# Loading the down-projection weights for their sums behind each pair's own weight loads, in a two-layer encoder step

## The chip, the cores and the metric

The kernel runs on one core of one Trainium2 chip. The metric is the device time of one launch in microseconds. The core has five engines with an instruction queue each: PE (TensorE, matmuls), DVE (VectorE), ACT (ScalarE), POOL (GpSimd) and SP (SyncE), which here issues all the transfers. Each engine works through its own list in the listed order and waits on semaphores for the others. A scheduler lays out these lists when the kernel is built: it follows the program's order and data dependencies, and an instruction may be moved ahead of others where the scheduler expects its inputs early.

## The reference, cut to what matters

Two layers, each an attention mixer followed by a channel mixer, for 1024 prompt positions and 8 x 16 sample positions (1152 rows of 1024 values). The change touches the channel mixer:

```python
def conv_ffn(h, prev, w_up, conv_w, conv_b, w_down):
    u = h @ w_up
    ...
    y = conv_b
    for tap in range(CONV_W):
        y = y + conv_w[tap] * ue[:, tap:tap + T]
    a, g = jnp.split(y, 2, axis=-1)
    out = (jax.nn.gelu(g) * a) @ w_down
    return out, ue[:, T:]
...
    f, conv_rows = conv_ffn(h, None if prompt else state_conv[l], w_up[l], conv_w[l], conv_b[l], w_down[l])
    x = layer_norm(DEEPNORM_ALPHA * x + (1 + g_f) * f, ln_g[l, 1], ln_b[l, 1])
```

`w_up` has 2 x 2816 columns, that is 22 blocks of 128 for `a` and 22 for `g`; `w_down` has 22 blocks of 128 rows. All data are float32; each operand is split into a rounded part and a remainder, so every product costs three matmuls.

## The kernel before, in words

`ffn(l, ...)` is the channel mixer of layer `l` and has two stages. The **up-projection** runs over 22 pairs `j` (block `j` of `a` with block `j` of `g`). The first two (`plain`) are ordinary products. The other twenty (`spair(j)`, j = 2 to 21) use a seven-product scheme over 2 x 2 quarters (`products`): POOL forms sums of weight quarters (lines 1177 to 1180), ACT and DVE split each of seven weight operands (lines 177 and 188), PE multiplies (line 1229, 24 matmuls for each product, 168 for a pair), and DVE adds the products up out of PSUM (line 1190), ACT for two of the seven (lines 1188 and 1197). The products of a pair share three groups of PSUM banks, and products 2, 3 and 4 share one: the matmuls of the second may start only when DVE has read the first. Then the convolution follows, `conv_row`, once for `g` and once for `a`: one ACT pass (line 1316), then two long and two short DVE operations, called taps here (line 1277), and a POOL addition (line 1286). `gated` applies GELU (line 1323, ACT), multiplies (line 1324, POOL) and stores the activations (lines 1326 and 1330). After every second pair `act_sums` forms four sums of stored activations on POOL (lines 1336 to 1339, called in the pair that follows) and stores both results (line 1341); the gate row that it stores is then overwritten by the next `conv_row`, which so waits for this store.

The **down-projection** (`down`, PE line 1466) is a seven-product scheme too, and needs sums of `w_down` quarters. `weight_sums(m)`, m = 0 to 10, makes them during the up-projection: two loads of 512 KB into the pair of tiles `w0f` (line 1347), four POOL operations on 128 x 512 (lines 1348 to 1351), and two stores to DRAM (line 1353). It is called in eleven of the twenty pairs: j = 2, 3 and every even j from 4 to 20. Nothing in the code ties a sum's loads to its pair: the tile `w0f` is free as soon as the last sum is stored, so the scheduler may pull the loads, and with them the sums, as far ahead as the tile allows.

In layer 0 the up-projection also carries 64 background steps (`ada`, four matmuls of 32 x 256 at line 234 each, with a 512 KB load at line 226), and at its start a small table (`tables_b`, load at line 1650, DVE lines 1651 and 1652) and sixteen transfers that spread it in DRAM (line 1657).

`down` ends with the last layer norm, tile of 128 rows by tile. The residual rows of a tile are loaded (`rows`, line 1081) into a buffer named in `homes`; in the table of before, tiles 2, 3, 6 and 7 use again the buffers `fa` and `fb` of earlier tiles, and a load waits until the earlier tile's output is stored (line 1019).

Names in the profile: `ws` and `F` hold weights as loaded (`F` is one large scratch tile with many uses), `wh` and `wl` the split weights, `H`, `xa` and `x2r` the split activations, `w0f` the pair of tiles for the down weights, `wT` and `actS` the stored sums, `actD` the stored activations, `PS` the PSUM banks.

Of the kernel before, what the change touches and what calls it, by code (L numbers as in the profile page):

```python
# [102 lines left out]
class Trunk:  # L103
# [1140 lines left out]
    def ffn(self, l, xsrc, xdst, affs):  # L1244
        nc, I, O, H, F = self.nc, self.I, self.O, self.H, self.F
# [67 lines left out]
        def conv_row(u, j, gg, y):  # L1313
            cc = j + 22 * gg
            tap = tapper(cc)
            nc.scalar.activation(y, u[:, 2:1154], AF.Identity, bias=cw[:, cc, 3:4], scale=cw[:, cc, 2:3])  # L1316
            tap(y[:, 0:1024], u[:, 1:1025], 1)
            tap(y[:, 0:1024], u[:, 0:1024], 0)
            samples(y[:, 1024:1152], u[:, 1026:1154], cc, tap)
            rows(j, gg, u[:, 1024:1168])  # L1320

        def gated(j, ya, yg):
            nc.scalar.activation(yg, yg, AF.Gelu_apprx_tanh)
            nc.gpsimd.tensor_mul(yg, yg, ya)  # L1324
            if j % 2:
                nc.sync.dma_start(self.actD[j], yg)
                self.pend.append(j // 2)
            else:
                for r in (slice(0, 512), slice(1024, 1152)):
                    nc.sync.dma_start(self.actD[j][:, r], yg[:, r])  # L1330

        def act_sums():
            for m in self.pend:
                a11, a21 = ygate[0][:, 0:512], ygate[0][:, 512:1024]
                a12, a22 = ygate[1][:, 0:512], ygate[1][:, 512:1024]
                nc.gpsimd.tensor_add(a22, a21, a22)
                nc.gpsimd.tensor_sub(a21, a11, a21)
                nc.gpsimd.tensor_sub(a11, a22, a11)
                nc.gpsimd.tensor_sub(a12, a12, a11)
                for i in range(2):  # L1340
                    nc.sync.dma_start(self.actS[m, i], ygate[i][:, 0:1024])
            self.pend = []

        def weight_sums(m):
            b11, b12, b21, b22 = (t[:, o : o + 512] for t in self.w0 for o in (0, 512))
            for i in range(2):
                nc.sync.dma_start(self.w0[i], I["wdn"][l, 2 * m + i])
            nc.gpsimd.tensor_sub(b11, b12, b11)
            nc.gpsimd.tensor_sub(b12, b22, b12)
            nc.gpsimd.tensor_sub(b22, b22, b11)  # L1350
            nc.gpsimd.tensor_sub(b21, b22, b21)
            for i in range(2):
                nc.sync.dma_start(self.wT[l][m, i], self.w0[i])
# [13 lines left out]
        def spair(j):  # L1367
            sa, sg = self.ws.next(), self.ws.next()
            nc.sync.dma_start(sa, I["wup"][l, j])
            nc.sync.dma_start(sg, I["wup"][l, j + 22])  # L1370
            ua, ug = us.next(), us.next()
            y = []

            def after(i, q):
                if i % 2 == 0:
                    self.step(1)
                if i == 1:
                    act_sums()
                if i == 2 and j in wsum:
                    weight_sums(wsum.index(j))  # L1380
                if q == 4:
                    y.append(ygate[j % 2])
                    conv_row(ug, j, 1, y[0])

            self.products(sa, sg, ua, ug, (S1, S2, S3), p1s, sub, TT, after, "first" if j == NPL else None)
            ya = yact
            conv_row(ua, j, 0, ya)
            gated(j, ya, y[0])

        self.pend = []  # L1390
        wsum = [2, 3] + list(range(4, NFF - 1, 2))
# [9 lines left out]
        for j in range(NPL, NFF):  # L1401
            spair(j)
            if l == 0 and j == 2:
                self.tables_b(self.ws.next())
            if l == 0 and 3 <= j < 19:
                with self.tc.issue_after(self.pairmm):
                    self.skew_b(j - 3)
# [4 lines left out]
    def down(self, l, xsrc, xdst, affs, act_sums):  # L1412
        nc, I, F, H = self.nc, self.I, self.F, self.H
# [13 lines left out]
        narrow = self.ws  # L1427
        fa, fb = F[:, 4096:5120], F[:, 8320:9344]
        homes = {8: fa, 0: fb, 1: self.w0[1], 2: fa, 3: fb, 4: X2[:, 0:1024], 5: X2[:, 2048:3072], 6: fa, 7: fb}
        xs = {}  # L1430

        def rows(*ts):
# [487 lines left out]
```

## Time and profile before

| what | us |
|---|---|
| median of three runs | 2839.86 |
| lowest and highest run | 2837.35 and 2843.75 |
| the profiled execution, own time | 2844.65 |
| the profiled execution, span from first to last instruction | 2842.6 |
| first and last load for a weight sum in the trace (line 1347, layers 0 and 1) | 515.8 and 2232.6 |
| first down-projection weight cast from `w0f` (line 177) | 1064.0 |
| first and last matmul of the twenty pairs of layer 1, about | 2075 and 2565 |

The mean granted TensorE clock of the profiled execution is 0.975 of full speed. Times inside the trace count from the start of the span; 2.05 us of the execution lie outside it. The table of windows in the prediction gives, for a stretch of time, each engine's busy time and in brackets its number of instructions, then the granted clock, the DMA share and the rate. A row of the timeline gives start, duration, engine, line, operation, operands and count, and in square brackets how long the engine had been idle before it and what ended that.

### The profile page before, as it was taken

What the parts mean: (1) busy time and instruction counts of PE and PEld (TensorE: products, weight loads), DVE (VectorE), ACT (ScalarE), POOL (GpSimd) and SP (SyncE); (2) the same over time, 40 slices, a digit from 0 to 9 for tenths busy, and PEclk for the clock granted to TensorE, in tenths of its full rate; (3) what the DMA queues carried; (4) which work ended last, traced back from release to release, by engine and by line L of the source; (5) the groups of instructions that cost most, each with busy time, mean ns of one, the idle gap of its engine ahead of it and who ended that gap; (6) DMA issues with size and microseconds to landing.
All of it is one profiled execution on the core that took longest, in us unless ns stands there. A gap on an engine that the chain in (4) does not pass through costs nothing. (4 is left out here: it accounts for less than half of the span.)

```text
span 2842.6 us, 47206 instructions
## 1 busy us (share of the span) xinstructions
PE 2676.1 (94%) x17134; PEld 2356.5 (83%) x17134; DVE 2027.0 (71%) x3850; ACT 1348.0 (47%) x2752; POOL 1106.9 (39%) x808
## 2 busy tenths in 40 slices
PE   7999889889999999999899999999988999999997
PEld 5897768878999997777798888767988999997775
DVE  4376767777776684588663677668888888885578
ACT  3475724433333344455636666652443344444454
POOL 2132523678554641013421111232489855551001
PEclk9999999999999999999999999999999999999998
DMA  8656434698554447675767457854565422237664
GB/s 291 213 159 197 141 129 156 209 329 283 183 175 156 163 133 236 225 248 196 267 201 257 122 156 198 225 162 146 178 206 196 177 81 96 85 116 239 216 218 156
DMA packets 252714, 534.35 MB, mean 188 GB/s; under 512 B 40032, under 2 KB 100400, under 8 KB 252480
## 3 DMA queue, kind: packets, MB, share of 16 engines
q1 hardware_dynamic: 252480, 531.32, 56.8%
q8 instruction: 135, 2.21, 0.3%
q14 instruction: 99, 0.81, 0.1%
HBM read 391.12 MB, written 149.54 MB: 190 GB/s over the span
## 5 line engine op out<-in xcount | busy, mean ns | idle before, releaser
L1229 PE MATMUL PS<-H,wh 128*128 128x256 f32 (+1 forms) x2624 | 409.7, 299 | 0.0
L1466 PE MATMUL PS<-wh,xa 128*128 128x512 f32 x1144 | 366.9, 399 | 11.9 <-DVE F L1584 5.3
L1229 PEld LDWEIGHTS PS<-H,wh 128*128 128x128 f32 x2624 | 374.4, 193 | 0.0
L1277 DVE SCALAR_TENSOR_TENSOR F<-F 128x1024 f32<-128x1024 f32 x320 | 312.9, 1025 | 28.1 <-ACT F L1316 27.8
L177 ACT CAST wh<-F 128x512 fp32r<-128x512 f32 (+2 forms) x234 | 137.1, 594 | 316.5 <-PE PS L1229 203.7
L1190 DVE TENSOR_TENSOR F<-PS,F 128x320 f32<-128x320 f32 (+1 forms) x446 | 196.6, 451 | 123.5 <-PE PS L1229 121.6
L188 DVE TENSOR_TENSOR wl<-F,wh 128x512 fp32r<-128x512 f32 (+2 forms) x234 | 238.6, 1029 | 56.0 <-ACT wh L177 54.3
L1466 PEld LDWEIGHTS PS<-wh,xa 128*128 128x128 f32 x1144 | 215.4, 189 | 69.5 <-ACT H L177 6.1
L1229 PE MATMUL PS<-H,wl 128*128 128x256 f32 (+1 forms) x1312 | 235.4, 301 | 24.4 <-ACT F L1197 15.3
L1466 PE MATMUL PS<-wl,xa 128*128 128x512 f32 x572 | 227.0, 397 | 0.2
L1229 PEld LDWEIGHTS PS<-H,wl 128*128 128x128 f32 x1312 | 196.6, 193 | 34.3 <-ACT F L1197 16.3
L1229 PE MATMUL PS<-xa,wh 128*128 128x320 f32 (+1 forms) x1328 | 207.5, 299 | 0.0
L188 DVE TENSOR_TENSOR xa<-xa 128x640 fp32r<-128x640 f32 (+1 forms) x154 | 122.5, 801 | 112.8 <-ACT xa L177 112.3
L1229 PEld LDWEIGHTS PS<-xa,wh 128*128 128x128 f32 x1328 | 189.8, 192 | 0.0
L1065 POOL TENSOR_TENSOR F<-F 128x1024 f32<-128x1024 f32 x24 | 62.7, 2611 | 308.2 <-ACT xa L177 148.9
L177 ACT CAST xa<-xa 128x640 fp32r<-128x640 f32 (+1 forms) x154 | 104.0, 682 | 162.8 <-DMA xa<-actD 110.8
L188 DVE TENSOR_TENSOR wl<-ws,wh 128x512 fp32r<-128x512 f32 (+1 forms) x149 | 166.2, 1120 | 10.3 <-ACT wh L177 10.2
L1316 ACT ACTIVATE F<-F 128x1152 f32<-128x1152 f32 x80 | 108.0, 1351 | 114.7 <-DVE F L1190 65.7
L177 ACT CAST wh<-ws 128x512 fp32r<-128x512 f32 (+1 forms) x167 | 113.1, 685 | 102.9 <-PE PS L1229 47.1
L640 POOL TENSOR_TENSOR F<-F,x2r 64x512 f32<-64x512 f32 x62 | 79.4, 1280 | 167.9 <-DVE F L616 145.6
L1324 POOL TENSOR_TENSOR F<-F 128x1152 f32<-128x1152 f32 x44 | 123.7, 2810 | 52.1 <-DVE F L1277 40.8
L1229 PE MATMUL PS<-xa,wl 128*128 128x320 f32 (+1 forms) x664 | 122.9, 307 | 21.2 <-DVE F L1190 20.7
(346 smaller groups left out, 6287.3 us busy)
## 6 DMA issues: line engine op xcount, KB each, us to landing
ws<-in_adaw_dram SPq DMA_DIRECT2D x64, 512.0 KB
ws<-in_wup_dram SPq DMA_DIRECT2D x49, 512.0 KB
F<-in_adaw_dram SPq DMA_DIRECT2D x48, 512.0 KB
w0f<-in_wdn_dram SPq DMA_DIRECT2D x44, 512.0 KB
wT<-w0f SPq DMA_DIRECT2D x44, 512.0 KB
actS<-F SPq DMA_DIRECT2D x44, 512.0 KB
xa<-actS SPq DMA_DIRECT2D x88, 256.0 KB
F<-in_wup_dram SPq DMA_DIRECT2D x39, 512.0 KB
```

Of the source, the lines that this page charges most:

```text
L177: nc.scalar.copy(out, in_)
L188: self.eng(el).tensor_sub(lo, src, hi.bitcast(F32))
L640: self.eng("v" if last else "p").tensor_mul(on[r, q], on[r, q], rb[r, :])
L1065: self.eng(er[0]).tensor_mul(xr, x, self.lng)
L1190: nc.vector.tensor_add(d, v(ps), a if len(a.shape) == 3 else v(a))
L1229: self.pairmm = nc.tensor.matmul(ps[:, 0:m], w[a][:, k * 128 : k * 128 + 128], x(p, k, n), start=start and c == 0, stop=c == 11, skip_grou ...
L1277: nc.vector.scalar_tensor_tensor(o, u, cw[:, cc, i : i + 1], o, op0=ALU.mult, op1=ALU.add)
L1316: nc.scalar.activation(y, u[:, 2:1154], AF.Identity, bias=cw[:, cc, 3:4], scale=cw[:, cc, 2:3])
L1324: nc.gpsimd.tensor_mul(yg, yg, ya)
L1466: self.downmm = nc.tensor.matmul(ps, a[p][:, i * 128 : i * 128 + 128], w[q], start=first and c == 0, stop=last and c == 2, skip_group_chec ...
```

## The change

Three edits. In `spair`, the second weight load of the pair is kept by name, and `weight_sums` is traced inside a block that places every instruction of SP traced there behind that load in SP's queue. The block adds no semaphore and touches no other engine; POOL's sums follow only because they need the loaded data. In `down`, for layer 1 alone, the residual rows of tiles 6 and 7 get buffers of their own, `self.hf` and `self.gateS`, in place of `fa` and `fb`.

```diff
@@ def spair(j)
             nc.sync.dma_start(sa, I["wup"][l, j])
-            nc.sync.dma_start(sg, I["wup"][l, j + 22])
+            pairdma = nc.sync.dma_start(sg, I["wup"][l, j + 22]).ins
...
                 if i == 2 and j in wsum:
-                    weight_sums(wsum.index(j))
+                    with self.tc.issue_after(pairdma):
+                        weight_sums(wsum.index(j))
@@ def down
         homes = {8: fa, 0: fb, 1: self.w0[1], 2: fa, 3: fb, 4: X2[:, 0:1024], 5: X2[:, 2048:3072], 6: fa, 7: fb}
+        if l:
+            homes[6], homes[7] = self.hf, self.gateS
```

The lists change almost only inside the two up-projections and at the end of layer 1. Lines up to 1369 keep their numbers; later lines move by one to three.

POOL in the second layer, in the middle of the up-projection, around the sums of stored activations. 1179, 1177, 1178 and 1180 are the next pair's weight sums. Before:

```order
L1286 TENSOR_TENSOR F<-F 128x8x2
L1324 TENSOR_TENSOR F<-F 128x1152
L1336 TENSOR_TENSOR F<-F 128x512
L1337 TENSOR_TENSOR F<-F 128x512
L1338 TENSOR_TENSOR F<-F 128x512
L1339 TENSOR_TENSOR F<-F 128x512
L1179 TENSOR_TENSOR F<-ws 128x512
L1177 TENSOR_TENSOR F<-ws 128x512
L1178 TENSOR_TENSOR F<-F,ws 128x512
```

The same place now:

```order
L1324 TENSOR_TENSOR F<-F 128x1152
L1348 TENSOR_TENSOR w0f<-w0f 128x512
L1349 TENSOR_TENSOR w0f<-w0f 128x512
L1350 TENSOR_TENSOR w0f<-w0f 128x512
L1336 TENSOR_TENSOR F<-F 128x512
L1351 TENSOR_TENSOR w0f<-w0f 128x512
L1337 TENSOR_TENSOR F<-F 128x512
L1179 TENSOR_TENSOR F<-ws 128x512
L1338 TENSOR_TENSOR F<-F 128x512
L1177 TENSOR_TENSOR F<-ws 128x512
L1339 TENSOR_TENSOR F<-F 128x512
L1178 TENSOR_TENSOR F<-F,ws 128x512
```

Between the gate product (1324) and the second half of the activation sums (1338) stood two operations, and now stand seven. This is repeated in every second pair; before, all eleven sums stood in the first pairs.

DVE in the same pair: the last read of the pair's products from PSUM (1190, 128x5x64 and 128x4x64 are the two halves of a product), the taps of both convolutions (1277), and the first read for the next pair. Before:

```order
L1190 TENSOR_TENSOR F<-PS,F 128x5x64
L1277 SCALAR_TENSOR_TENSOR F<-F 128x1024
L1277 SCALAR_TENSOR_TENSOR F<-F 128x8x15
L1190 TENSOR_TENSOR F<-PS,F 128x4x64
L188 TENSOR_TENSOR wl<-F,wh 128x512
L1277 SCALAR_TENSOR_TENSOR F<-F 128x1024
L1277 SCALAR_TENSOR_TENSOR F<-F 128x8x14
L1277 SCALAR_TENSOR_TENSOR F<-F 128x1024
L1277 SCALAR_TENSOR_TENSOR F<-F 128x8x15
L188 TENSOR_TENSOR wl<-F,wh 128x512
L1190 TENSOR_TENSOR F<-PS,F 128x5x64
```

The same place now:

```order
L1190 TENSOR_TENSOR F<-PS,F 128x4x64
L188 TENSOR_TENSOR wl<-F,wh 128x512
L1277 SCALAR_TENSOR_TENSOR F<-F 128x1024
L1277 SCALAR_TENSOR_TENSOR F<-F 128x8x15
L1277 SCALAR_TENSOR_TENSOR F<-F 128x1024
L1277 SCALAR_TENSOR_TENSOR F<-F 128x8x15
L1277 SCALAR_TENSOR_TENSOR F<-F 128x1024
L1277 SCALAR_TENSOR_TENSOR F<-F 128x8x14
L188 TENSOR_TENSOR wl<-F,wh 128x512
L1190 TENSOR_TENSOR F<-PS,F 128x5x64
```

Both reads of the pair's last product now stand ahead of all taps, and six taps in one block stand ahead of the next pair's first read.

SP in the second layer, the same pair. 1369 and 1370 are a pair's two weight loads. Before:

```order
L1370 DMA ws<-in_wup_dram 128x1024
L1326 DMA actD<-F 128x1152
L1369 DMA F<-in_wup_dram 128x1024
L1341 DMA actS<-F 128x1024 x2
L1370 DMA F<-in_wup_dram 128x1024
```

The same place now:

```order
L1370 DMA ws<-in_wup_dram 128x1024
L1347 DMA w0f<-in_wdn_dram 128x1024 x2
L1326 DMA actD<-F 128x1152
L1353 DMA wT_105<-w0f 128x1024
L1369 DMA F<-in_wup_dram 128x1024
L1353 DMA wT_105<-w0f 128x1024
L1341 DMA actS<-F 128x1024 x2
L1370 DMA F<-in_wup_dram 128x1024
```

The two loads follow the pair's own load, and the two stores of the sum now stand ahead of the next pair's first load and ahead of the activation sums' stores.

## The prediction, made before the changed kernel ran

> **What bounds the kernel now.** I read the page first, then the table of windows over both up-projections, then PE's waits in the bad windows, then single pairs in the timeline.
>
> ```profile
> span 2842.6 us, 47206 instructions
> ...
> PE 2676.1 (94%) x17134; PEld 2356.5 (83%) x17134; DVE 2027.0 (71%) x3850; ACT 1348.0 (47%) x2752; POOL 1106.9 (39%) x808
> ```
>
> PE is the bound: it is idle for 6% of the span. The question is how much of that idle time belongs to the sums of the down weights.
>
> ```profile
> core 0: us, PE busy (x) PEld busy (x) DVE busy (x) ACT busy (x) POOL busy (x), PEclk, DMA share, GB/s
> 560.00:620.00 60.00, 48.67 (x365) 44.13 (x364) 43.17 (x52) 19.09 (x32) 42.48 (x29) 0.91 0.90 326
> 620.00:760.00 140.00, 136.25 (x1062) 124.72 (x1062) 105.27 (x135) 48.54 (x83) 111.14 (x77) 1.00 0.75 256
> 760.00:1000.00 240.00, 240.00 (x1889) 220.93 (x1889) 169.45 (x247) 91.90 (x153) 128.89 (x94) 1.00 0.49 163
> 2100.00:2260.00 160.00, 140.10 (x971) 137.80 (x972) 144.24 (x151) 54.85 (x94) 141.84 (x90) 0.94 0.53 190
> 2260.00:2540.00 280.00, 280.00 (x2101) 279.88 (x2101) 239.28 (x312) 114.93 (x198) 165.12 (x113) 1.00 0.26 93
> ```
>
> The third and fifth rows are the quiet parts: PE never idles and the clock is 1.00. They give its pace, 1889/240 = 7.87 matmuls a us in layer 0 and 2101/280 = 7.50 in layer 1, so a pair of 168 matmuls takes 22.4 us there. At these paces the other rows should have taken 365/7.87 = 46.4, 1062/7.87 = 134.9 and 971/7.50 = 129.4 us. They lost 13.6, 5.1 and 30.6 us, 49.3 us together. POOL shows the difference: 142 of 160 us busy in the bad window of layer 1, 165 of 280 in the quiet one.
>
> ```profile
> L1348 POOL TENSOR_TENSOR w0f<-w0f 128x512 f32<-128x512 f32 x8 | 14.3, 1794 | 3.4 <-DMA w0f<-in_wdn_dram 3.4
> L1349 POOL TENSOR_TENSOR w0f<-w0f 128x512 f32<-128x512 f32 x9 | 16.6, 1850 | 1.0 <-DMA w0f<-in_wdn_dram 0.9
> PE PS L1229 <- DVE F L1190: 20.1, 10, 5.6
> L1277 DVE SCALAR_TENSOR_TENSOR F<-F 128x1024 f32<-128x1024 f32 x24 | 42.2, 1760 | 0.9 <-ACT F L1316 0.8
> L1277 DVE SCALAR_TENSOR_TENSOR F<-F 128x1024 f32<-128x1024 f32 x48 | 69.9, 1457 | 10.7 <-ACT F L1316 10.7
> ```
>
> The first four rows are of 2100 to 2260, the last of 2260 to 2540. Eight of layer 1's eleven sums run in these 160 us, some seven pairs. The only releaser of PE there is DVE reading PSUM (L1190), late ten times. DVE is late because its long taps (L1277) take 1.76 us there against 1.46 later, while POOL is full.
>
> ```profile
> 2153.00 1.43 PE L1229 MATMUL PS<-xa,wl 128*128 128x320 f32 x4 [5.58 <-DVE F L1190]
> 2179.80 0.85 PE L1229 MATMUL PS<-xa,wl 128*128 128x320 f32 x4 [1.43 <-DVE F L1190]
> ```
>
> A gap also costs afterwards: behind 5.58 us idle four matmuls take 1.43 us, behind 1.43 us idle 0.85. That is why 30.6 us are lost to 20.1 us of idle time, a factor of 1.52. The Trainium skill says the same under "TensorE: Matmul & The Clock Gate", What's actually happening: the clock drops to half after an idle window of about 3.4 us. By it, eight stalls of 2 us would carry no surcharge and cost 16 us; the two rows above agree.
>
> **The change part by part.** Removed: nothing. The 44 loads, 88 POOL sums and 44 stores stay, and so do all matmuls. What moves is when they run.
>
> *Layer 1.* The first three sums stand about where they stood, and I count nothing for them. The eight others, which cost 30.6/8 = 3.8 us of PE each, move to one in every second pair. Their new price must come from a pair of the quiet part:
>
> ```profile
> 2439.05 2.68 POOL L1324 TENSOR_TENSOR F<-F 128x1152 f32<-128x1152 f32 x1 [1.53 <-DVE F L1277]
> 2444.66 1.29 POOL L1336 TENSOR_TENSOR F<-F 128x512 f32<-128x512 f32 x1 [2.93 <-DMA actD<-F]
> 2447.39 1.62 POOL L1338 TENSOR_TENSOR F<-F 128x512 f32<-128x512 f32 x1
> 2449.04 1.70 SPq L1341 DMA_DIRECT2D actS<-F  x2
> 2451.77 1.35 ACT L1316 ACTIVATE F<-F 128x1152 f32<-128x1152 f32 x1 [1.86 <-DMA actS<-F]
> 2453.15 2.58 DVE L1277 SCALAR_TENSOR_TENSOR F<-F 128x1024 f32<-128x1024 f32 x2 [1.77 <-ACT F L1316]
> 2461.12 0.48 DVE L1190 TENSOR_TENSOR F<-PS,F 128x320 f32<-128x320 f32 x1
> 2461.72 0.50 PE L1229 MATMUL PS<-xa,wl 128*128 128x320 f32 x2
> ```
>
> This is a chain with almost no slack at its end: POOL's L1338, the store of the activation sums, ACT's convolution pass, DVE's taps, DVE's read of PSUM at 2461.12 to 2461.60, and PE, which wants that bank at 2461.72. The sum is put into its head. L1324 ends at 2441.75. Now eight operations run from there to the end of L1338 (1348, 1349, 1350, 1336, 1351, 1337, 1179, 1338). At 1.5 us each, between the 1.29 and 1.62 of these rows, L1338 ends at 2453.75 in place of 2449.0: a slip of 4.7 us, of which POOL's old idle time of 2.9 has already been used up. The first tap then starts at 2457.9. In the new order six taps, a split and the read follow: three long taps of 1.457 and three short ones between 0.3 and 0.85,
>
> ```profile
> L1277 DVE SCALAR_TENSOR_TENSOR F<-F 128x120 f32<-128x120 f32 x24 | 20.4, 852 | 0.0
> L1277 DVE SCALAR_TENSOR_TENSOR F<-F 128x112 f32<-128x112 f32 x24 | 7.8, 324 | 0.0
> ```
>
> that is 4.4 + 2.0 = 6.4, with about 0.7 for the split and 0.48 for the read 7.6 us: the read ends near 2465.5. PE's new order puts seven matmuls of another product (0.9 us) ahead of the blocked ones, so PE wants the bank at 2462.65. The stall is 2.9 us; with POOL at 1.29 for each of the eight the slip is 3.1 and the stall 1.3. Bounds: nothing, if the taps are quicker too, and the old 3.8; a loss beyond that is a rival below. I take 2.0 us, the middle of the chain's two ends, and no surcharge, since the row behind 1.43 us of idle time shows next to none. Eight of them cost 16, so layer 1 gains 30.6 - 16 = 14.6 us.
>
> What waits behind the new waits: on SP the first store of a sum stands ahead of the next pair's first load and waits for L1349, done about 2444.8; the second waits for L1351 and stands ahead of the activation sums' stores, which wait longer anyway. What covers a late load is the six slots of split weights: they let the splits run up to five products of 22.4/7 = 3.2 us ahead of PE, 16 us. The first weights of the down-projection go into `w0f` too and wait for the last sum's store, but that sum belongs to pair 20, more than a pair (22.4 us) ahead; if that lead were gone, PE would wait there for one load and one split, some 4 us in each layer (the load at 561.42 below lands in 2.5).
>
> *Layer 0.* A pair has the background steps too, and here the sum falls behind the third weight sum (L1178) of every second pair:
>
> ```profile
> 863.65 1.62 POOL L1180 TENSOR_TENSOR F<-ws,F 128x512 f32<-128x512 f32 x1
> 870.39 0.22 POOL L1286 TENSOR_TENSOR F<-F 128x16 f32<-128x16 f32 x1 [5.13 <-DVE F L1277]
> 876.22 0.49 DVE L1190 TENSOR_TENSOR F<-PS,F 128x320 f32<-128x320 f32 x1
> 881.30 0.85 PE L1229 MATMUL PS<-xa,wl 128*128 128x320 f32 x4
> ```
>
> POOL sits idle for 5.13 us just there, so four operations of 1.6 us are late by little more than 1 us, and DVE's read ends 4.6 us before PE wants the bank. The cover is enough: I price these sums at nothing, and if it were gone the price would be that of layer 1, 2.0 each. So the 5.1 us of 620 to 760 come back. Of the 13.6 us of 560 to 620 the sums are one cause of several:
>
> ```profile
> 560.99 0.33 SPq L1353 DMA_DIRECT2D wT<-w0f  x1
> 561.42 0.36 SPq L1650 DMA_DIRECT2D F<-in_relf_dram  x1
> 563.91 1.04 DVE L1651 TENSOR_SCALAR F<-F 16x257 f32<-16x257 f32 x1 [6.23 <-DMA F<-in_relf_dram]
> 609.82 1.44 PE L1229 MATMUL PS<-H,wl 128*128 128x320 f32 x4 [5.66 <-DVE wl L188]
> ```
>
> The table's load stood in SP's queue behind stores of sums and DVE waited 6.23 us for it; these stores now come later. The sixteen table transfers, with a DMA share of 0.90, stay. Bounds 0 and 13.6, I take half, 7. Layer 0 gains 12.
>
> *The end.* Tiles 6 and 7 no longer wait for an older tile's store.
>
> ```profile
> 2813.78 0.32 SPq L1081 DMA_DIRECT2D F<-xd  x1
> 2817.32 1.06 ACT L1530 ACTIVATE F<-F 128x1024 f32<-128x1024 f32 x1 [11.47 <-DMA F<-xd]
> 2818.91 3.66 PE L1466 MATMUL PS<-H,xa 128*128 128x512 f32 x15
> 2823.45 0.68 DVE L1618 TENSOR_TENSOR F<-F,PS 128x512 f32<-128x512 f32 x1
> 2825.64 5.41 POOL L1017 TENSOR_TENSOR x2f<-x2f,F 128x1024 f32<-128x1024 f32 x2 [38.73 <-ACT x2f L1016]
> 2826.02 2.83 DVE L1534 CUSTOM_DVE_ANT_0 F<-F 128x512 f32<-128x512 f32 x1
> ```
>
> ACT's scaling of tile 7 held up the statistics of tiles 4 and 5 by about 2 us. But PE works until 2822.57, and DVE's last subtraction at 2823.45 cannot start earlier: 0.9 us. POOL's multiplications, beside which L1534 takes 2.83 us, may fall a little earlier too. I take 1.5, bounds 0 and 4.
>
> Sum: 14.6 + 12 + 1.5 = 28 us. The profiled execution took 2844.65, 4.8 above the median, so it would take 2816.6, and the median goes from 2839.86 to about **2812**.
>
> **The rivals.** (1) *A sum costs the same wherever it stands.* For it: each POOL operation slows some DVE operation, early or late. Against it: the same density of sums lost 30.6 us in layer 1 and only 5.1 in layer 0's second window, so slack decides. Layer 1 would gain nothing, layer 0 only 7: with the end 8.5, so 2831. The Trainium skill would have it so: "SBUF — State Buffer", SBUF: two separate sides, calls the port pair of VectorE and GpSimd an exclusive lock, held for the whole instruction, so that lost time is not shared but conserved. The taps agree in part: slowed, but not by a whole POOL operation each.
>
> (2) *The gains come back in full.* All 49.3 and 2 at the end: 2789. For it: the quiet part has DVE idle for 41 of 280 us; against it the chain above, with 0.1 us of slack.
>
> (3) *Slower: the activation sums become the bound.* The place is the chain of layer 1. With POOL at the 1.85 us that L1349 takes when crowded, and some 2, L1338 ends near 2457, a slip of 8, and PE stalls by some 6 us in each of eight pairs; with the surcharge of 1.52 that is 73 us against 30.6, so 73 - 30.6 - 13.5 = 29 lost: 2869. It decides from 3.8 + 13.5/8 = 5.5 us lost for each sum, a slip of 5.4 with the surcharge and 7.3 without (the stall is the slip less 1.8).
>
> (4) *The sums don't spread, or it doesn't matter:* the background steps could keep layer 0 late, and the early sums were not what PE waited for; 2838. Against it speaks the one releaser in layer 1.
>
> **How the numbers follow.** The forecast, 2797 to 2829, has 0.53; (1) 0.15; (2) 0.14; (3) 0.13; (4) 0.05. What a measurement here can tell is about 0.2%, 5.7 us. Rival (1) at 8.5 us is just beyond it: 0.12 faster, 0.03 same. So faster 0.79, same 0.08, slower 0.13. The range leaves out (3) and half of (2), 0.20 in all, and reaches (4): 2793 to 2838.
>
> **What would show it.** Right: in the second layer no stretch of 160 us that lost 20 us; PE's waits on L1190 once in every second pair, 1 to 3 us each, at the matmuls behind the first product of a pair; ACT's L1316 waiting for actS by some 4 us more; in layer 0 no waits after 640, and L1651 waiting less; the last load of line 1081 long before 2800. Wrong: waits on L1190 of over 4 us in every second pair (rival 3) or none (rival 2); waits on the split weights (L188) or on DMA in the middle of either up-projection, which would mean that the stores in SP's queue hold up the pairs' loads.

## The result, and the profile after

| kernel | median us | runs | ratio to before, 95% interval |
|---|---|---|---|
| before | 2841.18 | 20 | |
| the change | 2836.03 | 20 | 0.9984 (0.9973 to 0.9995) |

The change gives some 5 us, under 0.2%. The forecast was 28. The profiled execution of the change took 2832.66 us with a span of 2830.8, 11.8 less than before's span; 5.7 of that had passed ahead of the first of the twenty pairs, in code that the change leaves alone, so spans of single executions are not compared here. What is compared is the time from the first to the last pair of a layer, taken at the first L1188 of each pair (nineteen intervals).

The first and last of these rows in layer 1, before:

```profile
2090.14 0.43 ACT L1188 COPY F<-PS 128x320 f32<-128x320 f32 x1 [2.77 <-PE PS L1229]
...
2550.06 0.43 ACT L1188 COPY F<-PS 128x320 f32<-128x320 f32 x1 [0.25 <-PE PS L1229]
```

And after:

```profile
2081.03 0.43 ACT L1188 COPY F<-PS 128x320 f32<-128x320 f32 x1 [2.87 <-PE PS L1229]
...
2541.05 0.43 ACT L1188 COPY F<-PS 128x320 f32<-128x320 f32 x1 [0.23 <-PE PS L1229]
```

That is 459.9 and 460.0 us: layer 1 gained nothing, where 14.6 were forecast. In layer 0 the same count gives 499.2 and 495.2. From the last pair to the end it is 292.5 and 289.8.

The table of windows of the change, with the same columns and stretches as in the prediction:

```profile
560.00:620.00 60.00, 51.43 (x399) 47.36 (x397) 40.66 (x52) 19.06 (x33) 45.12 (x31) 0.97 0.85 310
620.00:760.00 140.00, 140.00 (x1106) 128.27 (x1099) 104.17 (x141) 52.99 (x89) 93.16 (x64) 1.00 0.58 200
760.00:1000.00 240.00, 238.95 (x1870) 220.99 (x1869) 177.59 (x248) 89.65 (x153) 159.52 (x111) 1.00 0.60 202
2100.00:2260.00 160.00, 149.08 (x1090) 146.60 (x1089) 130.17 (x165) 60.97 (x106) 113.27 (x76) 0.99 0.37 131
2260.00:2540.00 280.00, 267.93 (x1990) 264.96 (x1990) 227.16 (x296) 111.62 (x190) 188.45 (x123) 1.00 0.36 129
```

At the paces of the prediction, the fourth row loses 160 - 1090/7.504 = 14.7 us (before 30.6) and the fifth 280 - 1990/7.504 = 14.8 (before nothing). The bad stretch is gone and its loss is spread, 29.5 for 30.6. Every two steady pairs took 44.8 us before:

```profile
2416.02 0.42 ACT L1188 COPY F<-PS 128x320 f32<-128x320 f32 x1
...
2460.81 0.42 ACT L1188 COPY F<-PS 128x320 f32<-128x320 f32 x1
```

After, they take 48.0, 3.2 us more for the one sum in them:

```profile
2424.18 0.43 ACT L1188 COPY F<-PS 128x320 f32<-128x320 f32 x1 [1.00 <-PE PS L1229]
...
2472.16 0.43 ACT L1188 COPY F<-PS 128x320 f32<-128x320 f32 x1 [1.01 <-PE PS L1229]
```

The waits in layer 1 after the change (engine, line, releaser: us in total, times, longest), from 2040 to 2600:

```profile
ACT F L1316 <- POOL F L1339: 34.5, 8, 5.2
...
PE PS L1229 <- ACT F L1197: 20.4, 8, 7.7
...
PE PS L1229 <- DVE F L1190: 10.8, 18, 1.7
```

Besides the releaser that the prediction named, L1190, there is another: ACT's read of product 11 out of PSUM, L1197. One pair of the timeline shows how it becomes late:

```profile
2438.97 1.35 ACT L1316 ACTIVATE F<-F 128x1152 f32<-128x1152 f32 x1
...
2439.16 1.79 POOL L1338 TENSOR_TENSOR F<-F 128x512 f32<-128x512 f32 x1
...
2440.35 2.97 DVE L1277 SCALAR_TENSOR_TENSOR F<-F 128x1024 f32<-128x1024 f32 x2 [0.56 <-ACT F L1316]
...
2440.92 2.27 POOL L1177 TENSOR_TENSOR F<-ws 128x512 f32<-128x512 f32 x1
...
2443.14 1.33 POOL L1339 TENSOR_TENSOR F<-F 128x512 f32<-128x512 f32 x1
...
2444.50 1.35 ACT L1316 ACTIVATE F<-F 128x1152 f32<-128x1152 f32 x1 [4.09 <-POOL F L1339]
...
2445.76 0.68 ACT L1197 COPY F<-PS 128x320 f32<-128x320 f32 x2
...
2445.88 3.95 DVE L1277 SCALAR_TENSOR_TENSOR F<-F 128x1024 f32<-128x1024 f32 x4 [2.56 <-ACT F L1316]
...
2446.21 0.85 PE L1229 MATMUL PS<-H,wl 128*128 128x320 f32 x4 [1.45 <-ACT F L1197]
...
2450.36 0.48 DVE L1190 TENSOR_TENSOR F<-PS,F 128x320 f32<-128x320 f32 x1
...
2457.30 0.86 PE L1229 MATMUL PS<-x2r,wl 128*128 128x320 f32 x4 [0.82 <-DVE F L1190]
```

The wide convolution pass of the gate (the second L1316) overwrites a gate row that the last activation sum, L1339, still reads. L1339 ends 20.3 us behind the pair's first L1188 (before: 12.3). ACT has waited 4.09 us for it, and behind that pass in ACT's queue stands L1197, which frees the banks for product 21. PE waits 1.45 us, and 0.82 further on for DVE's read.

ACT's two passes of the pair have also changed places, which the lists of POOL, DVE and SP did not show. Before, the gate's pass stood first (2451.77, waiting for the store of its row) and the other second:

```profile
2456.16 1.35 ACT L1316 ACTIVATE F<-F 128x1152 f32<-128x1152 f32 x1 [2.53 <-DVE F L1190]
```

Now the other stands first (2438.97) and the late one of the gate second (2444.50).

### The profile page after: what moved, and what is told of

It reads as the page before. It is cut to its first block, busy times and chain, and to the rows that moved or that the text cites. A ratio compares the mean times of both kernels' runs of the same rounds, so it can differ in the third digit from the quotient of the medians.

```text
span 2830.8 us, 47176 instructions
## 1 busy us (share of the span) xinstructions
PE 2662.1 (94%) x17134; PEld 2341.0 (83%) x17134; DVE 2000.5 (71%) x3850; ACT 1346.4 (48%) x2752; POOL 1116.0 (39%) x808
## 5 line engine op out<-in xcount | busy, mean ns | idle before, releaser
L1469 PE MATMUL PS<-wh,xa 128*128 128x512 f32 x1144 | 367.2, 399 | 12.7 <-ACT wh L177 3.7
L1277 DVE SCALAR_TENSOR_TENSOR F<-F 128x1024 f32<-128x1024 f32 (+1 forms) x320 | 304.8, 998 | 38.2 <-ACT F L1316 37.7
L188 DVE TENSOR_TENSOR wl<-F,wh 128x512 fp32r<-128x512 f32 (+2 forms) x234 | 244.6, 1053 | 84.7 <-ACT wh L177 76.6
L1190 DVE TENSOR_TENSOR F<-PS,F 128x320 f32<-128x320 f32 (+1 forms) x446 | 194.6, 449 | 109.5 <-PE PS L1229 107.8
L188 DVE TENSOR_TENSOR xa<-xa 128x640 fp32r<-128x640 f32 (+1 forms) x154 | 120.0, 784 | 111.2 <-ACT xa L177 110.4
L1316 ACT ACTIVATE F<-F 128x1152 f32<-128x1152 f32 x80 | 108.1, 1351 | 118.8 <-DVE F L1190 46.3
L1324 POOL TENSOR_TENSOR F<-F 128x1152 f32<-128x1152 f32 x44 | 125.0, 2841 | 77.9 <-DVE F L1277 30.2
L188 DVE TENSOR_TENSOR wl<-ws,wh 128x512 fp32r<-128x512 f32 (+1 forms) x149 | 146.6, 989 | 7.9 <-ACT wh L177 7.8
L306 PE MATMUL PS<-H,w0r 128*128 128x384 f32 (+1 forms) x720 | 138.2, 342 | 0.0
```

Source lines behind the costliest of these rows:

```text
L188: self.eng(el).tensor_sub(lo, src, hi.bitcast(F32))
L306: mm = self.nc.tensor.matmul(out[:, 0:n], w[a][:, k * 128 : k * 128 + 128], H[:, p, k, s0 : s0 + n], start=i == 0, stop=i == 23)
L1190: nc.vector.tensor_add(d, v(ps), a if len(a.shape) == 3 else v(a))
L1277: nc.vector.scalar_tensor_tensor(o, u, cw[:, cc, i : i + 1], o, op0=ALU.mult, op1=ALU.add)
L1469: self.downmm = nc.tensor.matmul(ps, a[p][:, i * 128 : i * 128 + 128], w[q], start=first and c == 0, stop=last and c == 2, skip_group_chec ...
```

## Experiments

Two theories. **A, the chain:** the sum stands ahead of the activation sums on POOL, the convolution pass waits for these, and PE waits for what stands behind that pass. **B, the conserved price:** a sum costs PE about the same wherever it stands, because POOL's work slows DVE's. The diffs are against the changed kernel. "Stretch" is the time from the first to the last pair of a layer; "price" is what two steady pairs of layer 1 take above 44.8 us.

**The parts alone.** Homes only; the placing in layer 0 only; the placing in layer 1 only:

```diff
-                    with self.tc.issue_after(pairdma):
-                        weight_sums(wsum.index(j))
+                    weight_sums(wsum.index(j))
```

> Only the buffers of tiles 6 and 7 at the end of layer 1 are changed; the sums run as before. In the two traces the stretch from the last pair of layer 1 to the end is 2.7 us shorter after the change (292.5 against 289.8). If that is the homes, this kernel is 1 to 3 us (0.05 to 0.1%) faster than before, and the up-projections take what they took before (499 us from the first to the last pair in layer 0, 460 in layer 1).

```diff
+                    if l == 0:
+                        with self.tc.issue_after(pairdma):
+                            weight_sums(wsum.index(j))
+                    else:
+                        weight_sums(wsum.index(j))
...
-        if l:
-            homes[6], homes[7] = self.hf, self.gateS
```

> Only layer 0 issues the loads behind each pair's own; layer 1 and the homes are as before. Both theories: layer 0 gives 4 to 6 us (499.2 to 495.2 from the first to the last pair in the traces), so 0.9980 to 0.9986 of before. Were it nothing, the gain of layer 0 in the traces would be chance between executions.

The third has `if l == 1` in the place of `if l == 0`.

> Only layer 1 issues the loads behind each pair's own; layer 0 and the homes are as before. Both theories: no change within 2 us, 0.9993 to 1.0007, since from the first to the last pair layer 1 took 459.9 us before and 460.0 after. My forecast had 14.6 us here, 0.995.

Measured: 0.9990 (0.9975 to 1.0005), 0.9986 (0.9972 to 1.0000) and 1.0008 (0.9992 to 1.0024), that is -2.8, -4.0 and +2.3 us, none beyond doubt by itself. They add up to -4.5, the change's own 0.9984. Stretches of layer 1: 457.4 and 457.4 with the old placing, 458.2 with the new. Layer 1 is worth nothing, as its trace had said.

**The sums in the other pairs.**

```diff
-        wsum = [2, 3] + list(range(4, NFF - 1, 2))
+        wsum = [2, 3] + list(range(4, NFF - 1, 2)) if l == 0 else [2] + list(range(3, NFF, 2))
```

> As the change, but in layer 1 the sums are called in pairs 2, 3, 5, 7 ... 21 in place of 2, 3, 4, 6 ... 20, so that from pair 5 on they fall into the pairs without sums of activations. Theory A (the chain: the sum stands ahead of the activation sums on POOL, the convolution pass on ACT waits for these, and ACT's read of PSUM stands behind that pass): the waits of PE on L1197 (20.4 us in 8) and on L1190 (10.8) all but go, the pairs of the steady part take 22.4 to 22.8 us in place of 24.0, layer 1 gains 20 to 27 us, ratio to before 0.989 to 0.992. Theory B (a sum costs PE its 3.2 us wherever it stands, since POOL's work slows DVE's): layer 1 stays at 460 us from the first to the last pair, ratio 0.998 as the change.

Measured: 0.9947 (0.9928 to 0.9965), 2826.01 us, and a stretch of 446.9. Waits of PE in layer 1:

```profile
PE PS L1229 <- DVE F L1190: 9.2, 25, 1.4
PE PS L1229 <- ACT F L1197: 9.1, 3, 7.7
```

One wait of 6 to 9 us at the start of the layer is there in every kernel; of the others on L1197, 9.1 - 7.7 = 1.4 us are left of 20.4 - 7.7 = 12.7. But the ratio lies between the two expectations. The price is 1.5: out of the chain, a sum costs 1.7 us less than 3.2, and the rest has another cause.

**The sums at the same place without POOL's work.**

```diff
-            nc.gpsimd.tensor_sub(b11, b12, b11)
-            nc.gpsimd.tensor_sub(b12, b22, b12)
-            nc.gpsimd.tensor_sub(b22, b22, b11)
-            nc.gpsimd.tensor_sub(b21, b22, b21)
```

> As the change, but POOL's four operations of each weight sum are left out in both layers; the loads and stores stay, so the stored tiles hold the loaded weights and the output is not the reference's. This prices all the sums at once. If POOL's work is what the sums cost, layer 1 falls from 460 us (first to last pair) to 426 to 432, near 19 pairs of 22.4, and layer 0 from 495 by 3 to 20; ratio to before 0.980 to 0.989. If the cost is in the loads and stores in SP's queue or in the DMA share, layer 1 stays above 445 and the ratio above 0.993.

Measured: 0.9903 (0.9880 to 0.9927); stretches 490.1 and 445.5. Layer 0 came out as expected. In layer 1 the stretch fits the second expectation (above 445) and the ratio neither: the price is 1.7 with no sum computed at all. The timeline shows why:

```profile
2408.93 0.33 SPq L1349 DMA_DIRECT2D wT<-w0f  x1
...
2409.35 0.38 SPq L1326 DMA_DIRECT2D actD<-F  x1
...
2413.38 1.76 POOL L1336 TENSOR_TENSOR F<-F 128x512 f32<-128x512 f32 x1 [5.00 <-DMA actD<-F]
...
2421.33 7.60 DVE L1277 SCALAR_TENSOR_TENSOR F<-F 128x1024 f32<-128x1024 f32 x6
...
2429.99 0.86 PE L1229 MATMUL PS<-xa,wl 128*128 128x320 f32 x4 [0.37 <-DVE F L1190]
```

(Lines from 1352 on have numbers four lower in this kernel.) The activations' store waited in SP's queue behind the store of a sum, the activation sums started after 5.00 us of idle time in place of 2.93, and all six taps again stood in one block ahead of DVE's read. So a delay of the activation sums costs by itself, whatever causes it, which speaks for A. One rival stays: here and in the change both last reads of a pair stand ahead of all taps in DVE's list, where in the runs with a price of 1.5 or less one of them stands between the taps, as before. No run kept the order of the lists while the activation sums were on time, so the order and the delay are not separated.

**The sums behind the activation sums, in the same pairs.**

```diff
+                self.lastact = nc.gpsimd.tensor_sub(a12, a12, a11).ins
...
+                    with ExitStack() as es:
+                        es.enter_context(self.tc.issue_after(pairdma))
+                        if l and j >= 4 and j % 2 == 0:
+                            es.enter_context(self.tc.issue_after(self.lastact))
+                        weight_sums(wsum.index(j))
```

> As the change, the sums in the same even pairs, but in layer 1 from pair 4 on POOL's four operations are placed behind the last activation sum (L1339) of that pair; all else is as in the change, so the same work in the same pairs. Theory A (chain): L1316 no longer waits for L1339 for 4 us, PE's waits on L1197 (20.4 us) go to under 3 beside the one of 7.7 at the start of the layer, layer 1 falls from 460 to 440 to 450, as with the odd pairs (446.9); ratio 0.993 to 0.996. Theory B (a sum costs the same in any place of the even pair, and the odd pairs are just roomier): 457 to 461, ratio 0.998.

Measured: 1.0100 (1.0070 to 1.0131), slower than before; stretch 481.7, price 6.4. Both theories missed. Its pair:

```profile
2408.23 1.35 ACT L1316 ACTIVATE F<-F 128x1152 f32<-128x1152 f32 x1 [2.56 <-DVE F L1190]
...
2408.92 1.75 POOL L1350 TENSOR_TENSOR w0f<-w0f 128x512 f32<-128x512 f32 x1
...
2409.43 6.08 DVE L1277 SCALAR_TENSOR_TENSOR F<-F 128x1024 f32<-128x1024 f32 x4
...
2413.13 2.24 POOL L1351 TENSOR_TENSOR w0f<-w0f 128x512 f32<-128x512 f32 x1
...
2415.43 1.75 DVE L188 TENSOR_TENSOR wl<-F,wh 128x512 fp32r<-128x512 f32 x1
...
2417.63 0.86 PE L1229 MATMUL PS<-xa,wl 128*128 128x320 f32 x4 [3.71 <-DVE F L1190]
...
2418.33 1.99 PE L1229 MATMUL PS<-xa,wh 128*128 128x320 f32 x8
```

The chain is gone as A says: the pass L1316 no longer waits for L1339, and L1197 is on time. But the sum now stands beside the four taps for which DVE has no slack. In the run with odd pairs the same block of four, with POOL idle for 2.92 us beside it, reads:

```profile
2439.43 4.00 DVE L1277 SCALAR_TENSOR_TENSOR F<-F 128x1024 f32<-128x1024 f32 x4
...
2443.36 0.68 DVE L188 TENSOR_TENSOR wl<-F,wh 128x512 fp32r<-128x512 f32 x1
```

Taps and split took 6.08 + 1.75 in place of 4.00 + 0.68: 3.2 us late, and PE stood for 3.71. The price of 6.4 is larger than this stall because the clock fell too: the mean granted clock from 2260 to 2540 was 0.95 in this run and 1.00 in the change. How POOL makes DVE late is seen when the block is read instruction by instruction:

```profile
2411.79 1.37 POOL L1178 TENSOR_TENSOR F<-F,ws 128x512 f32<-128x512 f32 x1
2411.91 2.33 DVE L1277 SCALAR_TENSOR_TENSOR F<-F 128x1024 f32<-128x1024 f32 x1
...
2415.33 1.29 POOL L1180 TENSOR_TENSOR ws<-ws,F 128x512 f32<-128x512 f32 x1
```

A long tap takes 1.27 us when POOL is idle. This one began while L1178 ran and ended 1.08 us behind L1178's end at 2413.16. L1351, next on POOL, ended 1.13 us behind the end of the tap at 2414.24, and it takes 1.29 otherwise. The split L188 began while L1180 ran and ended 0.56 behind it. So each waits for the instruction that runs on the other. B's mechanism is real, but its price depends on what stands beside the sum.

**The link through ACT cut.**

```diff
-                nc.scalar.copy(p1, ps[:, 0 : NB[n][3] - NB[n][2]])
+                (nc.vector.tensor_copy if self.evd else nc.scalar.copy)(p1, ps[:, 0 : NB[n][3] - NB[n][2]])
...
+        self.evd = l == 1
```

> As the change, but in layer 1 the copy of product 11 out of PSUM (L1197) is made by DVE in place of ACT, so that it no longer stands behind ACT's late convolution pass. If that copy's place on ACT alone is the cause, PE's stall of 1.5 us in every second pair goes, layer 1 gains 8 to 12 us, ratio 0.994 to 0.996. If the late pass holds PE through DVE as well (its taps stand ahead of the next read L1190 and end at the same time), the wait moves from L1197 to L1190 and layer 1 stays within 4 us of 460: ratio 0.997 to 0.9995; it may lose some, since DVE has the copy's 0.8 us to do in each pair.

Measured: 0.9988 (0.9968 to 1.0009), inside the second expectation; the first lies below the interval. The stretch of 453.3, price 1.9, lies between both. Its waits:

```profile
PE PS L1229 <- DVE F L1190: 19.3, 10, 2.9
PE PS L1229 <- DVE F L1197: 9.7, 2, 8.8
```

The waits on L1190 rose from 10.8 to 19.3 us in fewer and longer pieces: the late pass holds PE through DVE's taps as well. By the trace ACT's queue was worth 1.3 of the 3.2 us; 1.9 are left with DVE's end of the chain, which here has the copy to do as well.

**Odd pairs in both layers.** The list of the run with odd pairs, without its condition on the layer.

> As the run with odd pairs in layer 1, and layer 0 in odd pairs as well. In layer 0 the activation sums stand in the even pairs too, so if the same chain works there, the loss of layer 0 falls by some us: from 495 to 485 to 492 from the first to the last pair, ratio 0.992 to 0.994. If layer 0 has slack at this place (POOL idle 5 us ahead of its weight sums), nothing changes there and the ratio is 0.9947 again.

Measured: 0.9961 (0.9941 to 0.9982), by which it can't be told from the odd pairs in layer 1 alone (0.9947). The stretch of layer 0 is 503.6, worse by 8, and PE's waits on L1190 and L1197 from 760 to 1060 come to 10.2 us where the change has 3.9. The scheduler's list of POOL differs in layer 0:

```profile
831.34 1.28 POOL L1338 TENSOR_TENSOR F<-F 128x512 f32<-128x512 f32 x1
...
832.59 1.74 POOL L1348 TENSOR_TENSOR w0f<-w0f 128x512 f32<-128x512 f32 x1
...
835.54 1.74 POOL L1339 TENSOR_TENSOR F<-F 128x512 f32<-128x512 f32 x1
```

There the sum of an odd pair slips in among the next pair's activation sums. What counts is the place in POOL's list, not the pair that calls it; that this place alone makes the 8 us was not tested.

**A sum cut to fit two gaps of POOL, in layer 1.** `weight_sums` in three parts (loads; two operations; two operations and the stores); `lastgate` is POOL's L1324, and layer 1 calls `weight_sums` itself only for the first two sums:

```diff
+                if l and j > 3 and j % 2 == 0 and i == 0:
+                    with self.tc.issue_after(self.lastgate):
+                        weight_part(j // 2, 1)
+                if l and j > 3 and j % 2 and i == 0:
+                    with self.tc.issue_after(self.lastgate):
+                        weight_part(j // 2, 2)
+                if l and 3 <= j < 20 and j % 2 and i == 2:
+                    with self.tc.issue_after(pairdma):
+                        weight_part(j // 2 + 1, 0)
```

> As the change in layer 0 and at the end, but in layer 1 each sum from the third on is cut in two: two of POOL's operations stand in the even pair between L1324 and L1336, where POOL waits 2.9 us for the stored activations, and the two others in the odd pair between L1324 and L1179, where it waits 3.3 us; the loads follow the odd pair's own loads. If a sum costs nothing so long as it fits into a gap of POOL, the price falls from the 1.5 us of the odd pairs to 0 to 0.7, layer 1 takes 430 to 440 us from the first to the last pair in place of 446.9, ratio to before 0.991 to 0.9935. If what is left of the price is DVE slowed beside POOL wherever POOL works (rival), it stays 1.5 and the ratio 0.9945 to 0.9955.

**Layer 1 without sums.**

```diff
-        wsum = [2, 3] + list(range(4, NFF - 1, 2))
+        wsum = [2, 3] + list(range(4, NFF - 1, 2)) if l == 0 else []
...
-        wdn, wT, actD, actS = I["wdn"][l], self.wT[l], self.actD, self.actS
+        wdn, wT, actD, actS = I["wdn"][l], self.wT[0], self.actD, self.actS
```

> As the change, but layer 1 makes no weight sums at all: no loads, no POOL operations, no stores; its down-projection reads the stored sums of layer 0, so the output is not the reference's. This is the floor of layer 1. If the 1.7 us that a sum cost with POOL's work left out (two pairs took 46.5 us, against 44.8 without any sum) were its loads and stores in SP's queue, the steady pairs take 22.4 us each here, and layer 1 from the first to the last pair 428 to 434 us in place of 445.5; ratio to before 0.986 to 0.990. If that 1.7 us comes from elsewhere, it stays at 443 to 447, ratio 0.992 to 0.994.

Measured: the cut sum 0.9929 (0.9909 to 0.9949), a ratio inside my first expectation, but with a stretch of 445.6 and a price of 1.4: nearly all of the odd pairs' price is left, as the rival has it. The floor 0.9869 (0.9845 to 0.9893), stretch 431.6, price 0, as expected.

**Which part of the cut sum still costs.** The same kernel, POOL's operations only for layer 0 and the first two sums:

```diff
-                nc.gpsimd.tensor_sub(b11, b12, b11)
-                nc.gpsimd.tensor_sub(b12, b22, b12)
+                if l == 0 or m < 2:
+                    nc.gpsimd.tensor_sub(b11, b12, b11)
+                    nc.gpsimd.tensor_sub(b12, b22, b12)
```

and so for the other two.

> As the run with the sums cut in two, but in layer 1 POOL's four operations are left out from the third sum on (loads and stores stay, so the stored tiles hold the loaded weights and the output is not the reference's). Here the stores no longer stand ahead of the activations' store. The sum cut in two costs 1.4 us (two pairs take 46.2 us, 44.8 without any sum). If that is POOL's work beside DVE's, two pairs take 44.8 to 45.2 us, layer 1 431 to 436 us in place of 445.6, ratio to before 0.986 to 0.990. If it is the loads and stores, two pairs stay at 46.0 or more and layer 1 at 443 or more, ratio 0.992 to 0.994.

Measured: 0.9908 (0.9890 to 0.9927), stretch 434.7, price 0. Loads and stores cost nothing where no store stands ahead of the activations' store. What is left comes from POOL's four operations. DVE waits for them; the splits (L188) from 2260 to 2540, and ACT's wait for the store of the activation sums, cut sum:

```profile
L188 DVE TENSOR_TENSOR wl<-F,wh 128x512 fp32r<-128x512 f32 x59 | 67.7, 1155 | 4.4 <-ACT wh L177 4.4
L188 DVE TENSOR_TENSOR wl<-ws,wh 128x512 fp32r<-128x512 f32 x25 | 40.1, 1605 | 0.0
ACT F L1316 <- DMA actS<-F: 14.3, 5, 3.3
```

and its transfers alone:

```profile
L188 DVE TENSOR_TENSOR wl<-F,wh 128x512 fp32r<-128x512 f32 x58 | 57.0, 992 | 6.1 <-ACT wh L177 6.1
L188 DVE TENSOR_TENSOR wl<-ws,wh 128x512 fp32r<-128x512 f32 x26 | 39.0, 1500 | 0.0
ACT F L1316 <- DMA actS<-F: 5.6, 3, 1.9
```

59 splits slower by 0.163 us and 25 by 0.105 make 12.2 us in some twelve pairs, 2 us of DVE for each sum. The activation sums come later too, and ACT waits 14.3 us in place of 5.6. How the 1.4 divides between the two was not tested.

**The cut sum in both layers.** The same edit without `l and`.

> As the run with the sums cut in two, but in layer 0 as well. In layer 0 all sums together cost 5 to 6 us (496 us from the first to the last pair, 490.1 with POOL's operations left out). If a sum costs less in two gaps there too, layer 0 takes 491 to 495, ratio to before 0.990 to 0.9925. If layer 0's gaps lie elsewhere, or the odd place hurts as it did there (503.6), it takes 497 to 505, ratio 0.9935 to 0.996.

Measured: 0.9931 (0.9913 to 0.9950), median 2817.65 us, stretches 491.9 and 444.8. The trace agrees with the first expectation for layer 0. The ratio lies a little above it and is no better than with layer 1 alone (0.9929), so the gain of layer 0 is seen in the trace only. The kernel is clearly ahead of both kernels: its interval ends below that of the change (0.9973 to 0.9995).

Prices of a sum in the steady pairs of layer 1, by its place:

| place | price, us | stretch, us |
|---|---|---|
| no sum, or its transfers alone, clear of the activations' store | 0 | 431.6, 434.7 |
| cut into two gaps of POOL | 1.4 | 445.6 |
| odd pair, ahead of the next weight sums | 1.5 | 446.9 |
| as the change, POOL's work left out | 1.7 | 445.5 |
| as the change, product 11 read by DVE | 1.9 | 453.3 |
| as the change | 3.2 | 460.0 |
| even pair, behind the activation sums | 6.4 | 481.7 |

## Why the prediction was wrong

**What bounds the kernel: right.** With the sums away, the steady pairs stand at the quiet part's 44.8 us for two. But the 49.3 us that the windows lost were not all the sums'. By the runs without them the sums of before cost 459.9 - 431.6 = 28 us in layer 1 (26 by two other executions), and in layer 0 the mean of 499.2, 499.9 and 499.8 less 490.1, 9.5 us.

**Layer 1, +14.6 forecast, nothing measured. This is the step that failed:** "I take 2.0 us, the middle of the chain's two ends". The sum does stand in the head of the activation sums' chain, and PE does wait at its end, but the path to that end had a branch that I left out, and so the price was too low: 29.5 us were lost in the windows for eight sums, 3.7 each, 3.2 of it in the steady pairs, in place of 16 in all. Two links were wrong. First, I let the pass L1316 wait for L1338 and the store of its result; it waits for L1339, and L1338 and L1177 stand ahead of that in POOL's queue. From the start of L1324 to the pass it was 12.7 us before, 17.4 in my working, and is 19.4 (2425.07 to 2444.50): a slip of 6.7, not 4.7. L1338 itself ended 15.9 behind L1324's start, where the prediction had 14.7. This error hardly reached DVE's read, because a second one stood against it: only four of the six taps that I put behind the pass run there, and two ran ahead of it, from 2440.35. The read ended 25.8 us behind the start of L1324 (2450.84), where I had 26.4, and PE waited 0.2 us on it in the steady pairs (2450.89). That it came out so close is luck. Second, I followed DVE alone. ACT's queue behind the pass holds L1197, and PE waits on it first, 1.45 us; that link was not in the prediction. With product 11 read by DVE, where that branch is cut, the price is 1.9, close to my 2.0. A price higher by 1.7 us took nearly the whole gain, since the forecast lived on the difference of two prices close to each other, 3.8 and 2.0. The sign that I had named, no stretch of 160 us that lost 20 us, came out all the same: it could not tell 2.0 from 3.7.

**No surcharge: right for most of the new waits, but the reason was too simple.** The row behind the 1.45 us of idle time shows four matmuls in 0.85 us, and behind 2.17 us (2398.25) it is 0.85 too. Behind the one wait of 2.85 us (2253.68) the granted clock was 0.51 for 3.4 us. But in the trace of before the clock fell behind shorter waits as well:

```profile
2188.36 1.03 PE L1229 MATMUL PS<-x2r,wl 128*128 128x320 f32 x4 [1.87 <-DVE F L1190]
2209.38 1.44 PE L1229 MATMUL PS<-xa,wl 128*128 128x320 f32 x4 [2.68 <-DVE F L1190]
```

It was 0.50 from 2188.9 to 2192.3 and 0.51 from 2209.3 to 2212.7. In the run with the sums at the back, four matmuls took 0.86 behind 3.05 us of idle time (2368.92); behind 3.71 us the first four took 0.86 and the next eight 1.99, where they take 1.34 otherwise. "TensorE: Matmul & The Clock Gate" of the Trainium skill, What's actually happening, puts the drop of the clock behind idle windows of about 3.4 us. The 1.87 and 2.68 us are shorter than that, so the length of a single wait does not decide here, and eight stalls of 2 us might have carried a surcharge.

**Layer 0, +12 forecast, 4 measured.** The 5.1 of 620 to 760 came back in full (140.00 busy, 1106 matmuls for 1062). Of 560 to 620 came back 399 - 365 matmuls, 4.3 us for 7; DVE waited for the table 2.4 us in place of 6.23, as said. "I price these sums at nothing" did not hold: 760 to 1000 lost 240 - 1870/7.87 = 2.4 us that it had not lost before, and at 1019.08 PE waited 2.96 us for L1190, where before no wait from 760 to 1060 was over 0.3. And 12 was more than all the sums of the layer cost, 9.5. Eight executions with the new placing average 496.0, against 499.6.

**The end, +1.5 forecast, 2.7 in the trace and 2.8 by the run with the homes alone:** right within its bounds, though that run's interval does not exclude nothing. The last load of L1081 went out at 2768.73 (before 2813.78).

**The rivals.** (1) and (4) lie about equally near (2831 and 2838 for the measured 2836.03). (1) has layer 1 right, but for the wrong reason: a sum has not one price but prices from 1.4 to 6.4 us, so that the old place and the new came out alike (3.8 and 3.7) is chance. It leaned on the Trainium skill: "SBUF — State Buffer", SBUF: two separate sides, calls the shared port pair an exclusive lock, held for the whole instruction. The rows from 2411.79 to 2415.43 agree with it. But it does not follow that the price is conserved: DVE loses what is left of POOL's instruction, and PE feels it only where DVE has no slack. (2) falls: even with the chain gone 1.4 is left. (3) did not come with the change: in layer 1 no wait on L1190 was over 1.7 us. A loss of 1.0% came only with the sums behind the activation sums, and through DVE's taps. (4) is not it: the sums did spread. That 2836.03 lies inside the stated range, 2793 to 2838, is no merit of the sum, since the range was drawn to reach (4).

One pair in the middle of the change's trace took 26.6 us: there POOL's first operation of the sum waited 2.78 us for its load (0.76 in the pair shown), and PE waited 2.85 us on L1197, with the clock at half behind it. What stays open: why that load came late, and why it is some 30 us from the first to the second pair of layer 1 in every kernel, the one without sums too; no run was made for either.

## What to carry to other kernels

A side job on an engine that isn't the bound has no price of its own; its price is what stands behind it in that engine's list, and what comes up beside it on an engine that must wait for it, here DVE beside POOL. Spreading it helps only if the new place is cheaper, so price the new place first, link by link, through every queue that waits for it, to the last reader of the buffer that is overwritten. And where a gain is a difference of two prices, work out the floor (the job left out) before believing either: here it showed 28 us in layer 1, of which a better place brought 13 to 15.

## What was not expected of the hardware

DVE's long taps and POOL's operations do not slow each other little by little; each waits for the other's running instruction to end. In the run with the sums behind the activation sums, from 2100 to 2540, 43 long taps began while a POOL operation ran, and every one ended 1.08 to 1.12 us behind that operation's end, where a long tap alone takes 1.27. Of the splits of 128x512, 58 did so and ended 0.54 to 0.55 behind it; alone they take 0.68. POOL's 128x512 operations in their turn ended 1.12 to 1.16 us behind the end of the tap or split that they met, and take 1.29 alone. DVE's reads of PSUM (L1190, 128x320) did not wait: by the median they took 0.48 us alone and 0.49 beside a running POOL operation.
